# Decode steps that take keys and values together, and a fixed TensorE order beside the projections

## The chip, the cores and the metric

The kernel runs on one core of a Trainium2 chip. The metric is the time of one execution on the device in microseconds; the median of several executions counts, and less is better. TensorE (PE in the rows) multiplies matrices, its weight loads are listed apart as PEld; VectorE (DVE), ScalarE (ACT) and GpSimd (POOL) do the elementwise work; SyncE (SP) issues the DMAs, in order.

## The reference, cut to what matters

One layer of a streaming encoder, for 1024 prompt tokens and for a decode batch of 8 sequences with 16 new tokens each (128 rows that ride along as a ninth token tile). Group A has 8 heads of stick-breaking attention over the full past, group B 8 heads of softmax attention over the newest 512 past rows. The decode batch reads its past from caches in memory: 1024 rows of keys and as many of values for each sequence in group A, 512 in group B.

```python
q_a, k_a, v_a, q_b, k_b, v_b = split_heads(h, w_in)          # h = rmsnorm(x)
ka = jnp.concatenate([past_sb_k, k_a], axis=1)                # decode, group A
va = jnp.concatenate([past_sb_v, v_a], axis=1)
z = einsum('bqhd,bkhd->bhqk', q, k) * HEAD_DIM ** -0.5
log_keep = where(causal, log_sigmoid(-z), 0.0)
between = cumsum(log_keep, axis=3, reverse=True) - log_keep
w = where(causal, exp(log_sigmoid(z) + between), 0.0)
a = einsum('bhqk,bkhd->bqhd', w, v)
# group B: softmax(q k / 8 + relative bias) v; then per-head norms, the output
# projection, a SwiGLU feed-forward, a gated embedding and a final norm
```

## The kernel before

The kernel is one program whose stages are generators that call one another's steps. The projection `qkv` (L216) yields after each unit of 24 matmuls (8 blocks of the contraction by three products of high and low parts, `mm3`, L104). It goes through twelve column blocks of w_in: keys, queries and values of group A first, then keys, values and queries of group B. Its helper `others` (L244) handles keys and values: three token tiles of 24 matmuls each into one bank each of `ps["o"]`, a copy of each into `st`, and behind the third tile a tail: for keys six transposes (L260), the split into two parts and their writes; for values three casts and subtractions (`sv`, L264 to L268) and their writes; then the writes of the kernel's outputs. It yields after the first two tiles and after the tail.

`decode` (L314) is the other generator. Its setup loads the new queries, keys and values. Then it works through a list `seq` (L349 to L351) of pieces of 256 cached rows: key pieces and value pieces by turns, a batch's values following its keys by `nkc + VLAG` places (six in group A, three in group B). Group A has 32 key and 32 value pieces, group B 16 and 16. `fetch` loads a piece of 512 KB into one of seven buffers (six in group B), six (five) pieces ahead. `prepare` (L360) runs two pieces ahead: for keys eight transposes (L383) and two copies into `kT`, for values two transposes of the weights, three for a batch's first piece (`flip`, L389 to L394) and a copy into `wt`. `scores` (L397) multiplies four head pairs with 32 columns of queries each (L406) into one bank, `ps["s"]`; for the last piece of a batch in group A one matmul of 128 columns adds the causal mask (L409); two sigmoids on ScalarE read the bank. `weights` (L418) makes the scan and product on VectorE and the block `wn` of new weights on GpSimd. `outputs` (L440) multiplies two blocks of values (three for a batch's first piece) for four head pairs with 32 columns each (L449) into `acc`. Each fp32 matmul of 32 columns has two records in the trace, so a piece of keys shows 8 and a piece of values 16 or 24.

The order on each engine is set by a planner, which simulates the program and orders each engine's instructions ahead of time; on the chip every engine runs its own list in order. `tc.manual_schedule(engines=...)` makes the named engines keep the program's order instead. Before, decode's stages are all the planner's.

`advance(main, side, ratio, steps)` (L707) runs one step of `main` and then as many of `side` as the ratio makes due. The projection runs alone for 36 steps (L737). Group A's decode then runs beside 30 projection steps at 2.2 pieces per step (L747), and what is left of it runs out behind (L748). The stage's pools close, and prompt attention (`attention`, L492) starts beside the last 30 projection steps (L758). Group B's decode runs beside attention, and the embedding projection `embed` with it: `along` (L802) takes 0.55 embedding steps per decode piece, and attention takes 1.3 of both per step, for 40 steps (L816, L817).

Of the kernel before, what the change touches and what calls it, by code (L numbers as in the profile page):

```python
# [30 lines left out]
NEG = -1e30  # L31
LATE = 2
SKEW = 2
LAG, RAWS, PT = 5, 7, 2
VLAG, AHEAD = (2, 1), 2

# [2 lines left out]
def tile_hymba_step(  # L39
# [176 lines left out]
    def qkv(ch, hT, stg):  # L216
# [27 lines left out]
        def others(grp, w, c, wts, gs):  # L244

            wh, wl = wts
            for g in gs:
                st = stg.tile([P, 3, 256], F32, name="st", tag="st", bufs=2)
                for o in range(3):
                    ps_ = ps["o"].tile([P, 256], F32, name="ps", tag="O")  # L250
                    for k in range(KT):
                        mm3(ps_, *hT.tok(g * 3 + o, k), wh[:, k], wl[:, k], k == 0, k == KT - 1)
                    (V.tensor_copy if o % 2 else A.copy)(st[:, o], ps_)
                    if o < 2:
                        yield
                if w == 1:
                    for pr in range(2):
                        pt = ps["t"].tile([P, 384], F32, name="pt", tag="T")
# [21 lines left out]
                if g == 2:  # L280
# [1 line left out]
                        kv_sample[grp, w][0, :, :, c * 4 : c * 4 + 4, :].rearrange("b i h d -> (b i) (h d)"),  # L282
                        st[:, 2],
                    )
                yield

        loads = [(0, 1, 0), (0, 1, 1), (0, 0, 0), (0, 0, 1), (0, 2, 0), (0, 2, 1),
                 (1, 1, 0), (1, 1, 1), (1, 2, 0), (1, 2, 1), (1, 0, 0), (1, 0, 1)]
# [25 lines left out]
    def decode(grp, ch, dk):  # L314
# [79 lines left out]
            A.copy(wt, pt[:, : len(srcs) * P].rearrange("p (n m) -> p n m", m=P))  # L394
            return wt

        def scores(st, c, kT):  # L397
            last = c == nkc - 1
            nk = 272 if last else 256
            own = slice(c * 256, c * 256 + nk)  # L400
            q, w = st["q"], st["w"][:, own]
            sc = ps["s"].tile([P, 512], F32, name="sdec", tag="S")[:, :nk]

            masked = grp == 0 and last
            for pr in range(4):
                T.matmul(sc[pr * 32 : pr * 32 + 32], lhsT=q[:, pr], rhs=kT[:, pr, :nk], start=True, stop=not masked)  # L406
            if grp == 0:
                if masked:
                    T.matmul(sc[:, 256:], lhsT=identb, rhs=causalb, start=False, stop=True)  # L409
                A.activation(w, sc, AF.Sigmoid)  # L410
                A.activation(st["keep"][:, own], sc, AF.Sigmoid, scale=-1.0)
            else:
                mx = dk.tile([P, 1], F32, name="mx", tag="mx", bufs=4)
                V.tensor_tensor_reduce(w, sc, bias[:, own], 1.0,
                                       3e38 if st["mx"] is None else st["mx"], ALU.add, ALU.min, accum_out=mx)
                st["mx"] = mx
# [36 lines left out]
        def finish(st):  # L453
# [12 lines left out]
            V.tensor_scalar(ow, on, r[:, 0:1], None, op0=ALU.mult)  # L466
            nc.sync.dma_start(mixs[grp][b * 16 : b * 16 + 16, :].rearrange("i (h d) -> h i d", h=8), ow)

        ahead = ch.raws - 1
        for i in range(ahead):  # L470
            fetch(i)
        yield
        for i in range(AHEAD):
            prepare(i)
        for i, (kind, n, c) in enumerate(seq):
            if i + ahead < len(seq):
                fetch(i + ahead)
            if i + AHEAD < len(seq):
                prepare(i + AHEAD)
            x, wt = split.pop(i)  # L480
            if kind == "k":
                scores(batch[n], c, x)
                if c == nkc - 1:
                    weights(batch[n])
            else:
                outputs(batch[n], c, x, wt)
                if c == nkc - 1:
                    finish(batch[n])
            yield


# [252 lines left out]
    banks(dstack, "right", d=2, a=1)  # L744
    dp = pool(first, "dA", "left")
    dec = decode(0, Chunks(dp, "d", 1024, RAWS, 2), dp)
    advance(project, dec, 2.2, 30)  # L747
    for _ in dec:  # L748
        pass
    first.close()  # L750
    dstack.close()

# [49 lines left out]
    def along(a, b, ratio):  # L802

        due = 0.0
        for _ in a:
            yield
            due += ratio
            while due >= 1.0:
                due -= 1.0
                if next(b, "end") != "end":  # L810
                    yield
        yield from b

    next(dec)
    advance(att, dec, 0, 6)
    beside = along(dec, embed(), 0.55)  # L816
    advance(att, beside, 1.3, 40)  # L817
    for _ in beside:
        pass
    dstack.close()  # L820
# [655 lines left out]
```

## Time and profile before

| | us |
|---|---|
| median of three runs | 1763.65 (1763.17 to 1764.24) |
| the profiled execution | 1761.44 |
| its span, first to last instruction | 1759.7 |
| mean granted TensorE clock | 0.985 |
| TensorE busy | 1688.2 (96%) |
| VectorE busy | 1051.2 (60%) |
| GpSimd busy | 804.7 (46%) |
| ScalarE busy | 761.6 (43%) |

The profile is of one execution, with times in microseconds from its first instruction. Busy time counts an instruction from its start to its modelled end, so overlapping matmuls are seen best by their starts: the difference of two starts in the timeline is what an instruction costs TensorE. The timeline merges neighbours of one kind: "x8" are eight records. "128*32" says that the stationary operand has 128 rows and 32 columns. A bracket at a row's end is the idle time before it and what ended it. The granted clock is 1.00 for 2.4 GHz and 0.50 for 1.2 GHz, averaged over a stretch.

### The profile page before, as it was taken

To read this page: it belongs to the slowest core of one execution; us is meant where nothing else is said; L and a number is where in the kernel's file an instruction comes from. 1 tells how busy PE (TensorE), PEld (TensorE's weight loads), DVE (VectorE), ACT (ScalarE), POOL (GpSimd) and SP (SyncE) were. 2 spreads that over 40 slices of the span, in tenths; PEclk is the share of its full clock that TensorE was granted. 3 is DMA by queue.
4 is the path that set the end of the run, shared out by engine and by line. 5 is a ranking of instruction groups with operands and counts; after the bars stand their busy time and mean duration, and the time that the engine had idled before them with its cause. 6 is when DMAs were issued, how large, how long until landed. Compare 5 with 4: busy or idle time off the path is not lost.

```text
span 1759.7 us, 29028 instructions
## 1 busy us (share of the span) xinstructions
PE 1688.2 (96%) x11048; PEld 1469.3 (84%) x11048; DVE 1051.2 (60%) x1638; ACT 761.6 (43%) x1646; POOL 804.7 (46%) x635
## 2 busy tenths in 40 slices
PE   7999999999996899899989999999999999999998
PEld 7998888889995687787868888888888788887998
DVE  5212444257778566653686666666666598878635
ACT  5213434367766567743553333333233333333532
POOL 3214321277559322312345555555555465558354
PEclk9999999999998899999999999999999999999999
DMA  6756887656468696855422222222222684411123
GB/s 210 252 187 201 292 270 267 187 159 171 137 173 232 199 264 196 222 169 187 163 83 90 93 93 93 93 93 92 95 93 93 235 327 138 138 51 60 48 80 138
DMA packets 183467, 279.93 MB, mean 159 GB/s; under 512 B 15264, under 2 KB 115232, under 8 KB 181920
## 3 DMA queue, kind: packets, MB, share of 16 engines
q1 hardware_dynamic: 183328, 278.07, 49.4%
q8 instruction: 88, 1.44, 0.3%
q14 instruction: 51, 0.42, 0.1%
HBM read 198.47 MB, written 79.56 MB: 158 GB/s over the span
## 4 chain that ended last, share of the span: by engine, by line
PE 86%; DMA 4%; DVE 4%; POOL 3%; ACT 2%; issue 1%; SPq 0%; POOLq 0%; ACTq 0%; DVEq 0%
PE ps L998 19%; PE ps L105 9%; PE ps L106 9%; PE ps L107 8%; PE pt L1249 6%; PE ps L1249 4%; PE pt L998 3%; PE pt L584 3%; PE pt L383 2%; PE acc L449 2%; PE po L608 2%; PE po L607 2%; PE S L551 2%; PE sdec L406 1%; DMA v<-sv 1%
## 5 line engine op out<-in xcount | busy, mean ns | idle before, releaser
L110 POOL TENSOR_TENSOR wlo<-wraw,whi 128x512 fp32r<-128x512 f32 (+1 forms) x128 | 232.7, 1846 | 233.1 <-ACT whi L149 228.8
L105 PE MATMUL ps<-whi,hTh 128*128 128x256 f32 x576 | 168.9, 293 | 1.0 <-ACT sq L222 0.6
L106 PE MATMUL ps<-wlo,hTh 128*128 128x256 f32 x576 | 165.9, 288 | 1.0 <-POOL wlo L110 1.0
L107 PE MATMUL ps<-whi,hTl 128*128 128x256 f32 x576 | 166.6, 289 | 0.0
L149 ACT CAST whi<-wraw 128x512 fp32r<-128x512 f32 (+1 forms) x132 | 90.4, 749 | 98.0 <-PE ps L998 65.7
L565 DVE TENSOR_TENSOR_SCAN keep<-keep,zero 128x128 f32<-128x128 f32 (+4 forms) x64 | 100.9, 1585 | 38.5 <-ACT keep L557 37.8
L566 POOL TENSOR_TENSOR w<-w,keep 128x127 f32<-128x127 f32 (+4 forms) x64 | 89.2, 1405 | 66.4 <-DVE keep L565 57.9
L105 PEld LDWEIGHTS ps<-whi,hTh 128*128 128x128 f32 x576 | 110.9, 193 | 7.2 <-issue 5.0
L110 DVE TENSOR_TENSOR wtl<-pt,wth 128x512 fp32r<-128x512 f32 (+1 forms) x192 | 94.7, 514 | 32.0 <-ACT wth L588 31.1
L106 PEld LDWEIGHTS ps<-wlo,hTh 128*128 128x128 f32 x576 | 110.9, 192 | 3.2 <-issue 1.8
L107 PEld LDWEIGHTS ps<-whi,hTl 128*128 128x128 f32 x576 | 111.0, 193 | 0.3 <-issue 0.2
L584 PE MATMUL pt<-ident,w 128*128 128x128 f32 x528 | 92.0, 286 | 17.2 <-POOL w L566 13.5
L588 ACT CAST wth<-pt 128x512 fp32r<-128x512 f32 (+1 forms) x192 | 84.4, 464 | 37.8 <-PE pt L584 37.4
L584 PEld LDWEIGHTS pt<-ident,w 128*128 128x128 f32 x528 | 64.4, 146 | 27.1 <-POOL w L566 14.3
L105 PE MATMUL ps<-whi,hVh 128*128 128x256 f32 x288 | 81.8, 284 | 0.5 <-ACT hVh L1396 0.5
L106 PE MATMUL ps<-wlo,hVh 128*128 128x256 f32 x288 | 81.7, 284 | 0.0
L607 PE MATMUL po<-wth,vk 128*128 128x256 f32 (+1 forms) x304 | 80.7, 294 | 1.0 <-DVE wtl L110 1.0
L107 PE MATMUL ps<-whi,hVl 128*128 128x256 f32 x288 | 81.5, 284 | 0.0
L551 PE MATMUL S<-qk 128*128 128x384 f32 (+2 forms) x192 | 73.5, 385 | 4.7 <-DVE mxp L560 1.7
L608 PE MATMUL po<-wtl,vk 128*128 128x256 f32 (+1 forms) x304 | 77.0, 294 | 0.0
L384 DVE COPY kT<-pt 128x512 f32<-128x512 f32 x48 | 32.9, 688 | 65.9 <-PE pt L383 59.7
L110 POOL TENSOR_TENSOR actl<-actr,acth 128x1024 fp32r<-128x1024 f32 (+1 forms) x22 | 56.5, 2571 | 33.9 <-DMA sr<-acts 18.2
(351 smaller groups left out, 5402.6 us busy)
## 6 DMA issues: line engine op xcount, KB each, us to landing
draw<-in_cache_sb_k SPq DMA_DIRECT2D x32, 512.0 KB
draw<-in_cache_sb_v SPq DMA_DIRECT2D x32, 512.0 KB
act<-sg SPq DMA_DIRECT2D x11, 1152.0 KB
actr<-act SPq DMA_DIRECT2D x22, 576.0 KB
wraw<-in_w_in SPq DMA_DIRECT2D x12, 1024.0 KB
wraw<-in_w_gate SPq DMA_DIRECT2D x11, 1024.0 KB
wraw<-in_w_up SPq DMA_DIRECT2D x11, 1024.0 KB
v<-sv SPq DMA_DIRECT2D x36, 256.0 KB
```

The source lines that it names most:

```text
L105: T.matmul(out, lhsT=ah, rhs=bh, start=start, stop=False)
L106: T.matmul(out, lhsT=ah, rhs=bl, start=False, stop=False)
L107: T.matmul(out, lhsT=al, rhs=bh, start=False, stop=stop)
L110: eng.tensor_tensor(out, a, hi.bitcast(F32), op=ALU.subtract)
L149: A.copy(h[:, o], v[:, o])
L551: T.matmul(sc, lhsT=hd["qq"][:, qs], rhs=hd["kkh"][:, kc], start=True, stop=False)
L565: V.tensor_tensor_scan(rev, rev, zero[:, 0:1].to_broadcast([P, n]), 1.0, op0=ALU.mult, op1=ALU.add)
L584: T.transpose(pt[:, (c - c0) * P : (c - c0 + 1) * P], w[:, c * P : (c + 1) * P], ident)
L607: T.matmul(dst, lhsT=vs, rhs=wth[:, kb - base, c0:c1], start=(i == 0), stop=False)
L608: T.matmul(dst, lhsT=vs, rhs=wtl[:, kb - base, c0:c1], start=False, stop=(i == nkb - 1))
L998: T.matmul(out, lhsT=a[x][:, k], rhs=b[y][:, k], start=(not more and k == 0 and n == 0), stop=(k == 3 and n == 2), skip_group_check=more)
L1249: T.matmul(out, lhsT=a[i][:, x, m * P : (m + 1) * P], rhs=b[j][:, x], start=(not more and x == 0 and n == 0), stop=(x == 1 and n == 2), sk ...
```

## The change

Decode goes by steps instead of pieces: one place of the list, with a key piece, a value piece or both. In a step come the fetches, the preparations of the next step's pieces, scores and outputs, and then what follows a batch's last piece (`weights`, `finish`). The mask is added by four matmuls of 32 columns each. `others` yields behind each tile, the third one ahead of its tail. TensorE keeps the program's order in group A's decode stage. The ratios go from 2.2 to 1.2 (group A), from 0.55 to 1.0 and from 1.3 to 1.0 (group B).

```diff
+R2 = 1.2
...
                     (V.tensor_copy if o % 2 else A.copy)(st[:, o], ps_)
-                    if o < 2:
-                        yield
+                    yield
                 if w == 1:
...
-                yield
 
         loads = [(0, 1, 0), (0, 1, 1), (0, 0, 0), (0, 0, 1), (0, 2, 0), (0, 2, 1),
...
-        def scores(st, c, kT):
+        def scores(st, c, kT, _):
...
                 if masked:
-                    T.matmul(sc[:, 256:], lhsT=identb, rhs=causalb, start=False, stop=True)
+                    for pr in range(4):
+                        o = slice(pr * 32, pr * 32 + 32)
+                        T.matmul(sc[o, 256:], lhsT=identb[:, o], rhs=causalb, start=False, stop=True)
...
+        steps, at = [], 0
+        for pieces in zip_longest(ks, vs):
+            n = sum(x is not None for x in pieces)
+            steps.append(range(at, at + n))
+            at += n
         ahead = ch.raws - 1
         for i in range(ahead):
             fetch(i)
         yield
-        for i in range(AHEAD):
+        for i in steps[0]:
             prepare(i)
-        for i, (kind, n, c) in enumerate(seq):
-            if i + ahead < len(seq):
-                fetch(i + ahead)
-            if i + AHEAD < len(seq):
-                prepare(i + AHEAD)
-            x, wt = split.pop(i)
-            if kind == "k":
-                scores(batch[n], c, x)
+        for j, step in enumerate(steps):
+            for i in step:
+                if i + ahead < len(seq):
+                    fetch(i + ahead)
+            for i in steps[j + 1] if j + 1 < len(steps) else ():
+                prepare(i)
+            for i in step:
+                kind, n, c = seq[i]
+                (scores if kind == "k" else outputs)(batch[n], c, *split.pop(i))
+            for i in step:
+                kind, n, c = seq[i]
                 if c == nkc - 1:
-                    weights(batch[n])
-            else:
-                outputs(batch[n], c, x, wt)
-                if c == nkc - 1:
-                    finish(batch[n])
+                    (weights if kind == "k" else finish)(batch[n])
             yield
...
-    advance(project, dec, 2.2, 30)
-    for _ in dec:
-        pass
+    with tc.manual_schedule(engines={mybir.EngineType.PE}):
+        advance(project, dec, R2, 30)
+        for _ in dec:
+            pass
...
-    beside = along(dec, embed(), 0.55)
-    advance(att, beside, 1.3, 40)
+    beside = along(dec, embed(), 1.0)
+    advance(att, beside, 1.0, 40)
```

## Rows read from the trace of the kernel before

**Rows 1.** The page: busy time of each engine, and the chain that ended last, by engine.
```profile
PE 1688.2 (96%) x11048; PEld 1469.3 (84%) x11048; DVE 1051.2 (60%) x1638; ACT 761.6 (43%) x1646; POOL 804.7 (46%) x635
...
PE 86%; DMA 4%; DVE 4%; POOL 3%; ACT 2%; issue 1%; SPq 0%; POOLq 0%; ACTq 0%; DVEq 0%
```

**Rows 2.** Busy time by stretch: the stretch, its length, then each engine's busy time and instructions, the granted clock, the share of the DMA engines and GB/s. The first is group A's decode beside the projections, the last is group B's decode beside attention.
```profile
150.00:345.00 195.00, 192.13 (x2060) 163.59 (x2058) 70.85 (x101) 80.10 (x207) 54.57 (x72) 1.00 0.76 248
345.00:400.00 55.00, 51.15 (x380) 47.32 (x381) 32.92 (x38) 33.84 (x86) 35.27 (x27) 0.94 0.56 163
...
500.00:600.00 100.00, 78.93 (x566) 68.16 (x565) 68.04 (x106) 60.23 (x144) 61.00 (x54) 0.88 0.69 195
...
565.00:712.00 147.00, 136.84 (x1198) 108.89 (x1198) 92.90 (x292) 93.45 (x247) 42.55 (x69) 0.97 0.75 218
```

**Rows 3.** TensorE's timeline in group A's decode: the last projection matmuls before a stretch of scores, then a key piece and a value piece with their transposes, then the projection again; and two neighbouring groups of single transposes. Columns: start, length, engine, line, operation, out<-in, form, count.
```profile
154.57 0.28 PE L107 MATMUL ps<-whi,hTl 128*128 128x256 f32 x1
154.78 0.64 PE L406 MATMUL sdec<-kT,qbd 128*32 128x256 f32 x8
...
205.97 0.64 PE L406 MATMUL sdec<-kT,qbd 128*32 128x256 f32 x8
206.54 0.44 PE L392 MATMUL pt<-ident,wdec 128*128 128x128 f32 x2
206.91 0.64 PE L449 MATMUL acc<-draw,wt 128*32 128x128 f32 x16
207.49 0.39 PE L105 MATMUL ps<-whi,hTh 128*128 128x256 f32 x1
207.71 0.28 PE L106 MATMUL ps<-wlo,hTh 128*128 128x256 f32 x1
207.83 0.28 PE L107 MATMUL ps<-whi,hTl 128*128 128x256 f32 x1
...
212.09 0.27 PE L392 MATMUL pt<-ident,wn 128*128 128x128 f32 x1
212.20 0.38 PE L392 MATMUL pt<-ident,wdec 128*128 128x128 f32 x2
```

**Rows 4.** The same timeline where a value piece and a key piece follow each other with nothing between.
```profile
235.13 0.64 PE L449 MATMUL acc<-draw,wt 128*32 128x128 f32 x16
235.59 0.61 PE L406 MATMUL sdec<-kT,qbd 128*32 128x256 f32 x8
236.13 0.44 PE L392 MATMUL pt<-ident,wdec 128*128 128x128 f32 x2
```

**Rows 5.** The same timeline: two value pieces in one stretch, and the last stretch of group A's decode. From the one at 154.78 (rows 3) to this last one there are 60 stretches of 128*32 rows with 128*128 rows between them.
```profile
313.76 1.08 PE L449 MATMUL acc<-draw,wt 128*32 128x128 f32 x32
314.78 0.39 PE L105 MATMUL ps<-whi,hTh 128*128 128x256 f32 x1
...
323.85 1.08 PE L449 MATMUL acc<-draw,wt 128*32 128x128 f32 x32
```

**Rows 6.** The same timeline: a batch's last key piece with its mask.
```profile
219.77 0.67 PE L406 MATMUL sdec<-kT,qbd 128*32 128x272 f32 x8
220.37 0.18 PE L409 MATMUL sdec<-causalb,identb 128*128 128x16 bf16 x1
220.41 0.36 PE L105 MATMUL ps<-whi,hTh 128*128 128x256 f32 x1
```

**Rows 7.** TensorE's timeline in group B's decode: the first stretch, value pieces cut by attention's matmuls, and the last stretch. From the first to the last there are 42 stretches.
```profile
567.96 0.64 PE L406 MATMUL sdec<-kT,qbd 128*32 128x256 f32 x8
...
641.70 0.63 PE L449 MATMUL acc<-draw,wt 128*32 128x128 f32 x12
...
642.63 0.41 PE L449 MATMUL acc<-draw,wt 128*32 128x128 f32 x2
642.97 0.66 PE L584 MATMUL pt<-ident,w 128*128 128x128 f32 x4
...
709.44 0.42 PE L449 MATMUL acc<-draw,wt 128*32 128x128 f32 x6
```

**Rows 8.** Who waited for whom: total, times and longest in us. TensorE from 150 to 345, ScalarE from 140 to 345, TensorE from 345 to 400.
```profile
PE sdec L406 <- ACT keep L411: 1.5, 1, 1.5
...
ACT sv L267 <- DMA v<-sv: 13.4, 7, 4.6
...
PE pt L584 <- POOL w L566: 3.2, 1, 3.2
```

**Rows 9.** Timelines of TensorE, VectorE, GpSimd and ScalarE: a batch's masked scores, then its scan and its block of new weights; and the copy of a projection tile.
```profile
201.07 0.18 PE L409 MATMUL sdec<-causalb,identb 128*128 128x16 bf16 x1
...
202.01 2.33 DVE L424 TENSOR_TENSOR_SCAN keep<-keep,zero 128x1040 f32<-128x1040 f32 x1 [0.74 <-ACT keep L411]
...
205.77 0.20 POOL L437 COPY wn<-wdec 128x16 f32<-128x16 f32 x1 [3.77 <-DVE wdec L425]
...
205.21 0.37 ACT L253 COPY st<-ps 128x256 f32<-128x256 f32 x1 [2.96 <-PE ps L107]
```

**Rows 10.** Busy time by stretch of 20 us (columns as in rows 2): the one with the most DMA in group A's decode, and one at the start of attention.
```profile
200.00:220.00 20.00, 20.00 (x227) 16.00 (x229) 7.76 (x12) 9.79 (x25) 4.58 (x10) 1.00 0.92 312
...
360.00:380.00 20.00, 16.47 (x107) 14.89 (x106) 10.89 (x10) 12.24 (x31) 19.01 (x11) 0.83 0.44 139
```

**Rows 11.** Timelines of TensorE and SP from the end of group A's decode to attention's first matmul.
```profile
324.86 0.44 PE L260 MATMUL pt<-ident,st 128*128 128x128 f32 x2
325.05 0.36 PE L105 MATMUL ps<-whi,hTh 128*128 128x256 f32 x1
...
333.21 0.52 SPq L508 DMA_DIRECT2D qk<-qT0h  x1
...
342.83 0.47 PE L551 MATMUL S<-qk 128*128 128x128 f32 x2 [1.11 <-DMA qk<-kT0h]
```

## The prediction

> **What bounds the kernel now.** I read the page's busy table and chain first: TensorE is busy 96% of the span and carries 86% of the chain that ended last [rows 1]. Next the table by stretch: from 150 to 345 us, where group A's decode runs beside the projections, TensorE is busy 192.1 of 195 us at full clock; in group B's decode it is busy 136.8 of 147 [rows 2]. So an edit counts by TensorE time saved, if nothing new makes TensorE wait. Then TensorE's timeline shows what one decode step costs [rows 3]. Decode's matmuls write 32 partitions at a time (128*32 in the rows), everything else is 128*128, and going from one form to the other costs time that the rows show plainly.
>
> **The price of a stretch of 32-column matmuls.** A projection matmul starts every 0.12 us (207.71 to 207.83). After a stretch the first one takes 0.22 (207.49 to 207.71): 0.10 to leave. Before a stretch, the last one takes 0.21 (154.57 to 154.78): 0.09 to enter. Two transposes between two stretches take 0.37 (206.54 to 206.91), against 0.22 for two at 0.11 each (212.09 to 212.20 shows one): 0.15 for leaving and entering together. The stretch has a fixed part as well: eight score matmuls alone take 0.57 (205.97 to 206.54) and sixteen output matmuls alone 0.58, but both back to back take 1.00 (235.13 to 236.13), not 1.15 [rows 3, 4]. So each stretch that is joined to another saves 0.15 and one leaving and entering: 0.30 where transposes stood between, 0.34 where projection matmuls did. I take 0.32.
>
> **Group A.** By the program, before has 64 pieces (32 of keys, 32 of values). The timeline from the first to the last shows them in 60 stretches [rows 5]. In the change, 32 key pieces and 32 value pieces with six steps of lag make 38 steps, 26 of them with both. The order on TensorE is now the program's: next step's transposes first, then scores, then outputs, so 38 steps are 38 stretches, and 37 as nothing stands between the last two. 23 fewer at 0.32: **-7.4 us**.
>
> The mask: eight times, one 128*128 matmul of 16 columns (0.04 from 220.37 to 220.41, the leaving is paid behind it anyway) becomes four of 128*32 [rows 6]. A 32-column matmul of 16 columns is not in the trace. Nearest rows: sixteen more output matmuls in one stretch cost 1.02 - 0.58 = 0.44, 0.027 each [rows 3, 5], so four cost 0.11, and 8 x (0.11 - 0.04) = **+0.6**. Ends: -0.3 if they cost nothing; +2.4 if each four cost 0.34, as a stretch of two output matmuls by itself does (642.63 to 642.97) [rows 7]. I take +0.6, since they stand inside a stretch. The rows say 0.027 us for one more tile in a stretch. The Trainium skill's page "TensorE: Matmul & The Clock Gate", section "Measured speedup vs the span model", gives about 4 ns for a further tile of a packed group; by that the masks would cost some 0.1 us in all and not 0.9, an estimate from that page, and the sum would be 0.8 us lower. The measured row decides here.
>
> The fixed order: nothing else may fill when TensorE's next instruction waits. What is late next? (a) Scores need kT, copied one step earlier, and the one score bank, freed by two sigmoids; today one such wait of 1.5 us is left in the whole stage [rows 8]. (b) The first output step of a batch needs scan, product and wn: 202.01 to 205.97, 4.9 us after the masked scores end at 201.1 [rows 9]. The change leaves the rest of a step, at least one projection step (24 x 0.12 = 2.9 us) and another decode step (ten transposes at 0.11, 1.0 and 0.2 for entering and leaving: 2.3) before the flip that reads it: some 5.7 us, enough but barely when two decode steps follow each other. (c) Outputs now precede the scan's emission, which costs that chain 0.5 us of its room. (d) ScalarE waits 13.4 us in seven pieces for the DMA that frees a v tile, the longest 4.6 [rows 8]; behind such a wait stand the copies of kT and wt and the sigmoids, and TensorE waits for those. A decode step and a projection step (5 us) cover the single wait; without that cover it is TensorE's. Bounds 0 and 13.4; I take **+1.5**, the wait that the stage shows today, since the planned order is already close to the program's there [rows 3, 4].
>
> The moved yield: the third block's transposes (L260), its split and its DMAs on SP now come behind a decode step instead of in front of it. On TensorE this gives the copy of the third PSUM block (0.4 us) [rows 9] 2.3 us of cover that the fixed order would otherwise have lacked; on SP the cache fetches of that step go ahead of the block's writes. Who waits: v's sample rows for new_v, first needed by the first output step, six steps later. Zero, and at most the 1.5 above if the cover goes.
>
> Ratio 2.2 to 1.2: 30 projection steps take 35 advances, setup and 34 steps; four value-only steps follow alone at about 0.95 us each (0.37 + 0.58). It is TensorE work that before did between projections, so it costs nothing by itself. DMA demand rises with the shorter stage: its share is 0.76 over the stage and 0.92 in the worst 20 us [rows 2, 10], and 195 us less 5 raises it by 3%. Zero, above 1.0 in the worst slice only.
>
> **Group B.** 19 steps stand for 32 pieces, and the trace shows 42 stretches: the planner cuts output groups into twos and sixes with attention matmuls between [rows 7]. There TensorE's order stays the planner's. Kept whole: 23 fewer, -7.4. All cut again: 0. I take eleven fewer, about half: the pieces fall from 32 to 19, but the attention work that cuts them is still there, and for 10 us of this stretch TensorE idles anyway [rows 2]. 11 x 0.32 = **-3.5**. The ratios 0.55/1.3 to 1.0/1.0: 38 decode and embedding steps over 40 attention steps instead of 51 single ones; the same keys and values per attention step, zero.
>
> **The stage changes.** Between 345 and 400 TensorE idles 3.9 us and from 500 to 600 21 us with the clock at 0.88 [rows 2]: waits for POOL and DMA that a new plan will shuffle. After group A's last output (324.86) attention's first loads are issued at 333.21 behind the write of the last decode result, and its first matmul starts at 342.83; six projection steps fill TensorE till then [rows 11]. They are still there after the change. Zero, bounds -4 and +4 (about the 3.9 of the first).
>
> **Sum.** -7.4 + 0.6 + 1.5 - 3.5 = -8.8 us. The profiled execution takes 1761.44 (span 1759.7 and 1.7 around it): 1752.6. The median of the runs lies 2.2 higher, so 1763.65 - 8.8 = **1754.9**, with its own range 1750 to 1760.
>
> **Rivals.** *Fixed order turns ScalarE's waits into TensorE's* (slower). Place: projection steps 37 to 48, whose v blocks make ScalarE wait for DMA. All 13.4 us arrive and TensorE falls to the lower clock level: in 360 to 380 us a wait of 3.2 us for POOL goes with a granted clock of 0.83, 6.8 us at 1.2 instead of 2.4 GHz, 3.4 us lost [rows 8, 10]. -7.4 + 0.6 + 13.4 + 3.4 - 3.5 = +6.5: 1770. It decides against the change once more than 10.3 us of waits come through. For: order can't adapt, one score bank. Against: the order of before is nearly the same and waits 1.5 us. The Trainium skill's page "TensorE: Matmul & The Clock Gate", section "HAM oscillation — how this bites in real kernels", says the same of a TensorE that idles between bursts; the slice with 0.83 agrees. Chance 0.14.
>
> *The gain of A is given back at the stage change* (no change). The four value-only steps push decode's end behind the last projection step; if the plan doesn't hoist projection steps over attention's loads, up to 18 us (324.86 to 342.83) lie open, of which some 5 would eat A's net 5.3; with B at 0 to -3.5 the time is 1760 to 1764, 1762 in the middle. It would be the same if the change didn't do what it says, that is, if transposes came to lie between scores and outputs again; in A the fixed order speaks against that, in B nothing does. Chance 0.18.
>
> *B joins fully and waits shrink*: -7.4 + 0.6 - 7.4, less 1.5 us of waits that go: -15.7, 1748. For: steps emit scores and outputs together. Against: the cuts in [rows 7]. Chance 0.14. The forecast keeps 0.54.
>
> **Chances.** A measurement can tell about 0.2%, 3.5 us. Faster by more: forecast and full join, 0.68; within: 0.18; slower: 0.14. The range leaves out half of the slower case and the far end of the full join: 1746 to 1767.
>
> **What would show it.** In the profile after: 37 stretches in group A's decode, each with sdec directly followed by acc in about 1.0 us (1.2 with nv); four small masks inside; TensorE busy all through; the stage (first sdec to attention's first S) about 5 us shorter. In B, fewer acc groups of two and six. Wrong if TensorE shows new waits for ACT or DVE in A, if sdec and acc back to back still take 1.15, or if what A gains is lost between 340 and 600.

## The result, and the profile after

| | before | after |
|---|---|---|
| median, us | 1763.41 (1762.86 to 1764.24, 4 runs) | 1752.72 (1748.87 to 1754.20, 4 runs) |
| ratio, with 95% interval | | 0.9936 (0.9918 to 0.9953) |
| profiled execution; its span | 1761.44; 1759.7 | 1754.20; 1752.4 |
| mean granted TensorE clock | 0.985 | 0.984 |

The change is faster by 10.7 us; the forecast was 8.8. The profiled execution of after is the slowest of its four, and that of before lies below its four, so their spans differ by less, 7.3. The page of after, busy time by engine and the chain that ended last, by engine [rows 1]:

```profile
PE 1678.7 (96%) x11072; PEld 1470.8 (84%) x11072; DVE 1048.3 (60%) x1638; ACT 764.0 (44%) x1646; POOL 806.1 (46%) x635
...
PE 84%; DMA 5%; DVE 4%; ACT 2%; POOL 2%; issue 1%; SPq 1%; POOLq 0%; DVEq 0%; ACTq 0%
```

TensorE is busy 9.5 us less, with 24 more records (8 masks of four instead of one). It has more instructions and needs less time, which is what the price of a stretch says.

TensorE's timeline of after: a whole step, a masked step, and the last stretch of group A's decode [rows 3, 5, 6]:

```profile
215.17 1.03 PE L382 MATMUL pt<-ident,draw 128*128 128x128 f32 x8
216.04 0.27 PE L391 MATMUL pt<-ident,wn 128*128 128x128 f32 x1
216.15 0.38 PE L391 MATMUL pt<-ident,wdec 128*128 128x128 f32 x2
216.46 0.64 PE L405 MATMUL sdec<-kT,qbd 128*32 128x256 f32 x8
216.92 0.62 PE L450 MATMUL acc<-draw,wt 128*32 128x128 f32 x16
217.47 0.38 PE L106 MATMUL ps<-whi,hTh 128*128 128x256 f32 x1
...
305.39 0.67 PE L405 MATMUL sdec<-kT,qbd 128*32 128x272 f32 x8
305.87 0.19 PE L410 MATMUL sdec<-causalb,identb 128*32 128x16 bf16 x4
305.90 0.62 PE L450 MATMUL acc<-draw,wt 128*32 128x128 f32 x16
306.45 0.39 PE L106 MATMUL ps<-whi,hTh 128*128 128x256 f32 x1
...
322.73 1.08 PE L450 MATMUL acc<-draw,wt 128*32 128x128 f32 x32
```

Scores and outputs lie together: from 216.46 to 217.47 it is 1.01 us, as the prediction read it from the rare neighbours in before (1.00). From the first stretch at 156.40 to the last at 322.73 there are 37, the number forecast. The masked step costs 1.06, four masks included: they take 0.03 us, from 305.87 to 305.90.

Where the 7.3 us between the two spans arise, by the same events in each trace:

| | before | after | difference so far |
|---|---|---|---|
| attention's first matmul | 342.83 | 334.68 | -8.2 |
| group B's first scores | 567.96 | 558.12 | -9.8 |
| group B's last output matmul starts | 709.6 | 697.8 | -11.8 |
| end of the span | 1759.7 | 1752.4 | -7.3 |

So 8.2 us come in group A's stage, 1.7 from there to group B's decode, 2.0 in its stage, and 4.5 are given back later, in this execution. Two more profiles of the changed kernel, below, keep the first part (334.90, 335.42) and give back 1.2 and 4.2.

Who waited for whom: TensorE, and then ScalarE, in group A's stage of after (total, times, longest) [rows 8]:

```profile
PE pt L382 <- ACT kT L383: 0.7, 2, 0.5
PE pt L382 <- DVE kT L383: 0.6, 1, 0.6
PE pt L382 <- DVE sq L111: 0.3, 1, 0.3
...
ACT sv L267 <- DMA v<-sv: 6.9, 4, 2.3
```

TensorE's three waits make 1.6 us. ScalarE still waits for the DMA that frees v, 6.9 instead of 13.4 us, and nothing of it reaches TensorE: the last of these waits ends at 151.41, ahead of the first copy into kT at 154.63.

Busy time by stretch of after, columns as in [rows 2]: group A's stage, the start of attention, and group B's stage:

```profile
150.00:345.00 195.00, 193.06 (x2150) 171.80 (x2148) 73.24 (x110) 84.69 (x214) 50.90 (x70) 1.00 0.81 258
345.00:400.00 55.00, 51.88 (x402) 48.49 (x402) 37.14 (x43) 39.45 (x102) 43.77 (x32) 0.97 0.63 185
555.00:699.00 144.00, 133.05 (x1174) 108.61 (x1174) 91.77 (x284) 91.48 (x242) 37.89 (x66) 0.94 0.76 219
```

In group A's stage TensorE idles 1.9 of 195 us, as the waits say. At the start of attention the granted clock is 0.97 instead of 0.94; in group B's stage it is lower than before, 0.94 for 0.97. What is given back lies partly at the far end. The same view of a stretch of 70 us that begins 160 us ahead of the end, in before, in after, and in another execution of the changed kernel (after_again):

```profile
1600.00:1670.00 70.00, 67.84 (x425) 60.85 (x424) 50.29 (x73) 29.74 (x61) 38.54 (x32) 1.00 0.12 36
```

```profile
1592.00:1662.00 70.00, 67.82 (x415) 60.69 (x413) 49.62 (x72) 29.22 (x59) 37.36 (x32) 0.98 0.10 32
```

```profile
1586.00:1656.00 70.00, 67.84 (x422) 60.64 (x420) 51.01 (x73) 29.81 (x60) 38.94 (x33) 1.00 0.11 32
```

The granted clock is 1.00, 0.98 and 1.00. 0.02 of 70 us is 1.4 us of the 3.3 by which after's rest is longer than after_again's.

### The profile page after: what moved, and what is told of

Same layout as the page of the kernel before. It is cut to its first block, busy times and chain, and to the rows that moved or that the text cites. A ratio compares the mean times of both kernels' runs of the same rounds, so it can differ in the third digit from the quotient of the medians.

```text
span 1752.4 us, 29092 instructions
## 1 busy us (share of the span) xinstructions
PE 1678.7 (96%) x11072; PEld 1470.8 (84%) x11072; DVE 1048.3 (60%) x1638; ACT 764.0 (44%) x1646; POOL 806.1 (46%) x635
## 3 DMA queue, kind: packets, MB, share of 16 engines
q8 instruction: 88, 1.44, 0.3%
## 4 chain that ended last, share of the span: by engine, by line
PE 84%; DMA 5%; DVE 4%; ACT 2%; POOL 2%; issue 1%; SPq 1%; POOLq 0%; DVEq 0%; ACTq 0%
PE ps L1005 19%; PE ps L106 9%; PE ps L107 9%; PE ps L108 9%; PE pt L1256 6%; PE ps L1256 5%; PE pt L1005 3%; PE pt L590 3%; PE pt L382 2%; PE po L614 2%; PE S L557 2%; PE po L613 2%; PE acc L450 1%; PE sdec L405 1%; PE S L558 1%
## 5 line engine op out<-in xcount | busy, mean ns | idle before, releaser
L111 DVE TENSOR_TENSOR wtl<-pt,wth 128x512 fp32r<-128x512 f32 (+1 forms) x192 | 94.0, 513 | 24.2 <-ACT wth L594 23.5
L383 DVE COPY kT<-pt 128x512 f32<-128x512 f32 x48 | 33.0, 688 | 57.0 <-PE pt L382 46.5
```

The source lines that it names most:

```text
L111: eng.tensor_tensor(out, a, hi.bitcast(F32), op=ALU.subtract)
```

## The experiments

The theory from the prediction: the time comes from 32-column matmuls that lie together, about 0.32 us for each stretch saved, and TensorE's fixed order matters only as it keeps them together. The rivals: the fixed order or the later yield brings the time by itself; group B brings it; or what A gains is lost at the stage change. The runs came in three groups of four, each beside runs of before on the same chip: 1763.78 us (17 runs) for after_again, flip_between, planner_a and fixed_only, 1762.72 (17) for a_only, old_yield, wide_mask and fixed_b, 1764.30 (11) for the others. Each time is a median with its range and count. "Stretches" counts those of 128*32 rows in the profiled execution, in group A / group B (before: 60 / 42). "First S" is attention's first matmul there (before: 342.83; after: 334.68).

| run | us | ratio to before (95%) | stretches | first S |
|---|---|---|---|---|
| after_again | 1751.42 (1748.20 to 1751.88, 5) | 0.9929 (0.9916 to 0.9941) | 37 / 33 | 334.90 |
| after_third | 1751.47 (1749.70 to 1756.82, 6) | 0.9930 (0.9913 to 0.9947) | 37 / 33 | 335.42 |
| flip_between | 1761.14 (1759.08 to 1764.11, 11) | 0.9985 (0.9977 to 0.9994) | 63 / 33 | 343.78 |
| planner_a | 1751.12 (1748.92 to 1753.09, 5) | 0.9930 (0.9916 to 0.9944) | 49 / 33 | 337.31 |
| fixed_only | 1771.72 (1767.49 to 1774.75, 6) | 1.0044 (1.0029 to 1.0059) | 63 / 42 | 355.67 |
| pairs_only | 1755.82 (1754.43 to 1757.74, 6) | 0.9950 (0.9935 to 0.9965) | 67 / 33 | 346.02 |
| a_only | 1756.07 (1751.96 to 1757.28, 5) | 0.9953 (0.9940 to 0.9965) | 37 / 41 | 336.58 |
| old_yield | 1755.85 (1753.33 to 1762.13, 5) | 0.9951 (0.9938 to 0.9963) | 37 / 33 | 348.48 |
| wide_mask | 1749.67 (1748.07 to 1751.02, 4) | 0.9922 (0.9909 to 0.9935) | 44 / 33 | 336.31 |
| wide_mask_again | 1752.80 (1751.37 to 1756.87, 6) | 0.9936 (0.9920 to 0.9952) | 44 / 33 | 337.37 |
| fixed_b | 1766.73 (1757.88 to 1772.06, 12) | 1.0018 (1.0003 to 1.0032) | 37 / 19 | 335.33 |
| double_a | 1774.98 (1769.09 to 1778.18, 6) | 1.0054 (1.0034 to 1.0074) | 20 / 33 | 352.44 |

### The changed kernel again (after_again, after_third)

No edit. These stand beside the others of their group.

> The changed kernel once more, as the measure for the others on the same chip. Both theories: 1752.7 us, between 1748.9 and 1754.2 as its runs showed, 10.7 below before.

> The changed kernel, as the measure for this call: 1752, between 1748 and 1755.

The medians are 12.4 and 12.8 us below before. In group A they repeat within 0.8 us (first S at 334.68, 334.90, 335.42); behind group B's decode (whose last matmul starts at 697.8, 695.1, 696.1) the three spans still differ, 1752.4, 1746.4 and 1750.3. The part from there to the end takes 1054.6, 1051.3 and 1054.2 us, and 1050.1 in before. It is not the change's own: fixed_only, whose decode goes by pieces like before's, takes 1054.3 there, and flip_between and planner_a 1051.8 and 1051.4. In all fourteen profiles the clock of the stretch shown above is 1.00 in the four where this part is shortest (before, after_again, planner_a, flip_between; 1050.1 to 1051.8) and 0.98 in the other ten (1051.8 to 1055.2). So differences of some 5 us between single profiled executions mean nothing unless one stage shows them.

### Same steps, transposes between scores and outputs (flip_between)

```diff
-            for i in steps[j + 1] if j + 1 < len(steps) else ():
+            todo = list(steps[j + 1]) if j + 1 < len(steps) else []
+            for i in [i for i in todo if grp or seq[i][0] == "k"]:
                 prepare(i)
-            for i in step:
+                todo.remove(i)
+            for x, i in enumerate(step):
+                if todo and (x or len(step) == 1):
+                    prepare(todo.pop())
...
+            for i in todo:
+                prepare(i)
```

> The changed kernel with one move: in group A's steps with both pieces the next value piece's transposes stand between scores and outputs. Same instructions, same fixed order otherwise, 63 stretches of 32-column matmuls instead of 37. Joined stretches pay: 26 x 0.30 = 7.8 us slower than the changed kernel, 1760.5, attention's first matmul 7 to 8 us later (342). The fixed order pays by itself, or the stage changes were merely shuffled well: no difference of more than 2 us from the changed kernel, 1753.

Group A keeps its steps, fixed order, ratio and yield; only the two or three transposes of the weights move from ahead of the scores to behind them. TensorE's timeline of flip_between:

```profile
218.42 0.64 PE L405 MATMUL sdec<-kT,qbd 128*32 128x256 f32 x8
218.99 0.33 PE L391 MATMUL pt<-ident,wn 128*128 128x128 f32 x1
219.15 0.38 PE L391 MATMUL pt<-ident,wdec 128*128 128x128 f32 x2
219.46 0.64 PE L450 MATMUL acc<-draw,wt 128*32 128x128 f32 x16
220.04 0.39 PE L106 MATMUL ps<-whi,hTh 128*128 128x256 f32 x1
```

The same work lies in two stretches: 0.57 and 0.58 us instead of 1.01 together, and the first transpose behind scores takes 0.16 (218.99 to 219.15) instead of 0.11. There are 26 stretches more, and attention starts 8.9 us later than in after_again: 0.34 each. TensorE waits 2.7 us in this stage instead of 1.6; without these 1.1 it is 0.30 each, the figure of the expectation. The median, 1761.14, is the expected time within a microsecond; it is 9.7 us above after_again's, where 7.8 were expected. The run also says what the rest of the change is worth in group A: with 63 stretches first S is at 343.78; before has 60 and 342.83, three more stretches at 0.32 are 1.0, and the waits are alike (2.7, and 2.6 in before [rows 8, 11]). Fixed order, ratio and yield together come to nothing there.

### The planner's order in group A's stage (planner_a)

```diff
-    with tc.manual_schedule(engines={mybir.EngineType.PE}):
-        advance(project, dec, R2, 30)
-        for _ in dec:
-            pass
+    advance(project, dec, R2, 30)
+    for _ in dec:
+        pass
```

> The changed kernel without the fixed order in group A's decode stage. Joined stretches pay: the planner finds scores and outputs of a step ready together and keeps most of them together, since before it made only 60 stretches of 64 pieces; 38 to 44 stretches, 0 to 2 us slower than the changed kernel, 1752.7 to 1755. The fixed order pays by itself: most of the gain of group A is lost, 1759 to 1761, with waits of TensorE in the stage.

As fast as the changed kernel. TensorE's timeline of planner_a, one step that the planner cuts and one that it leaves whole:

```profile
250.75 0.64 PE L405 MATMUL sdec<-kT,qbd 128*32 128x256 f32 x8
251.32 0.66 PE L382 MATMUL pt<-ident,draw 128*128 128x128 f32 x4
251.90 0.64 PE L450 MATMUL acc<-draw,wt 128*32 128x128 f32 x16
...
257.14 0.64 PE L405 MATMUL sdec<-kT,qbd 128*32 128x256 f32 x8
257.60 0.62 PE L450 MATMUL acc<-draw,wt 128*32 128x128 f32 x16
```

The number of stretches was missed: 49, where 38 to 44 were expected. In the stage this shows, as first S comes 2.4 us later than in after_again: twelve stretches more at 0.32 are 3.8, and the 1.6 us of waits under the fixed order are gone, since TensorE is busy for 195.0 of 195 us here; that makes 2.2. In the median (1751.12 against 1751.42) it does not, and the ranges overlap. So the fixed order is not needed for the result; at most it is worth a couple of microseconds in its own stage.

### The fixed order alone (fixed_only)

The kernel before, with one edit:

```diff
-    advance(project, dec, 2.2, 30)
-    for _ in dec:
-        pass
+    with tc.manual_schedule(engines={mybir.EngineType.PE}):
+        advance(project, dec, 2.2, 30)
+        for _ in dec:
+            pass
```

> The kernel before, with TensorE's order fixed in group A's decode stage and nothing else. Joined stretches pay: 60 stretches become 63 or 64, 3 x 0.3 = 1 us, and the tail of a key block, no longer behind a decode step, makes TensorE wait for a copy (0.4 us and the signals, six times in keys): 1764 to 1768, not faster than before. The fixed order pays by itself: 1755 to 1758.

Slower by 7.9 us, and by more than expected. TensorE's waits in group A's stage of fixed_only:

```profile
PE pt L383 <- ACT kT L384: 3.8, 1, 3.8
PE pt L383 <- DVE sq L110: 2.2, 2, 1.4
PE pt L392 <- POOL wn L437: 1.5, 2, 0.8
PE pt L260 <- ACT st L253: 1.2, 5, 0.2
```

The longest, 3.8 us up to 156.81, is what the prediction's slower rival described. ScalarE's timeline shows its copy into kT right behind casts that waited for the DMA that frees v (3.58 us, and 1.44 once more):

```profile
152.50 0.41 ACT L267 CAST sv<-st 128x256 fp32r<-128x256 f32 x1 [3.58 <-DMA v<-sv]
155.87 0.40 ACT L267 CAST sv<-st 128x256 fp32r<-128x256 f32 x1 [1.44 <-DMA v<-sv]
156.18 0.58 ACT L384 COPY kT<-pt 128x512 f32<-128x512 f32 x1
```

A low clock went with it, as the rival had it: from 140 to 165 us the granted clock is 0.86, where before has 1.00; 0.14 of 25 us is 3.5 us, some of it while TensorE waited. The other waits are shorter: the program's order leaves too little between a copy or a block of new weights and TensorE's use of it. With the changed kernel's steps and its yield the same fixed order waits 1.6. First S is 12.8 us later than before; three more stretches make 1.0 of it, the waits 7.1 (8.7, and 1.0 of attention's first matmul for its load, less the 1.5 and 1.1 that before has there [rows 8, 11]) and the clock up to 3.5. Some 1 to 2 us stay unassigned.

### Only the steps (pairs_only)

Of the whole change only the steps and the ratios stay: the planner's order, the yield behind the tail and the wide mask of before.

```diff
-    with tc.manual_schedule(engines={mybir.EngineType.PE}):
-        advance(project, dec, R2, 30)
...
+    advance(project, dec, R2, 30)
...
+                    if o < 2:
+                        yield
...
+                yield
...
-                    for pr in range(4):
-                        o = slice(pr * 32, pr * 32 + 32)
-                        T.matmul(sc[o, 256:], lhsT=identb[:, o], rhs=causalb, start=False, stop=True)
+                    T.matmul(sc[:, 256:], lhsT=identb, rhs=causalb, start=False, stop=True)
```

> The change without the fixed order, without the moved yield and with the wide mask: the steps and the ratios alone, all orders the planner's. Joined stretches carry the change: 1752 to 1755, at least three quarters of the gain. The moved yield is needed even under the planner: 1756 or more.

The median is at the edge between the two expectations, and the trace decides. In group A the planner has 67 stretches, more than before, and first S is at 346.02, 3.2 us later than before: nothing is gained there. TensorE has no waits in the stage; seven more stretches (2.2) and eight more projection matmuls ahead of first S (1.0), less the 2.6 us of waits of before, explain 0.6 of the 3.2. TensorE's timeline of pairs_only shows how outputs are cut:

```profile
235.02 0.62 PE L450 MATMUL acc<-draw,wt 128*32 128x128 f32 x10
235.57 0.66 PE L384 MATMUL pt<-ident,draw 128*128 128x128 f32 x4
236.16 0.41 PE L450 MATMUL acc<-draw,wt 128*32 128x128 f32 x2
```

The last two output matmuls cost 0.34 (236.16 to the next row of transposes at 236.50), where two inside a stretch cost 0.05. What pairs_only gains comes from group B and the stage change, where its 33 stretches are those of the changed kernel; from first scores to last outputs group B takes 132.9 us, before 141.6. That steps are emitted together is not enough in group A: something must keep them whole. Between planner_a's 49 and these 67 lie two edits, the yield and the mask, and which of them keeps the planner's steps whole was not separated.

### Group A alone (a_only)

Group B goes by pieces again, with the old loop and the old ratios.

```diff
+        if grp:
+            for i in range(AHEAD):
+                prepare(i)
+            for i, (kind, n, c) in enumerate(seq):
+                if i + ahead < len(seq):
+                    fetch(i + ahead)
...
+                yield
+            return
...
-    beside = along(dec, embed(), 1.0)
-    advance(att, beside, 1.0, 40)
+    beside = along(dec, embed(), 0.55)
+    advance(att, beside, 1.3, 40)
```

> The changed kernel with group B's decode as before: pieces by turns, ratios 0.55 and 1.3. Joined stretches pay in both groups: group B goes from 33 stretches back to about 42, 9 x 0.32 = 2.9 us slower than the changed kernel, 1755 to 1756. Only group A's part counts, since TensorE idles in group B's stretch anyway: no difference, 1752.7.

Faster than before by 6.7 us, with group B's 41 stretches. Group B's stage takes 143.6 us here and 141.6 in before; with the steps it takes 139.7, 136.3 and 136.9 in the three profiles of the changed kernel. So the steps in B, with their ratios, are worth about 4 us or more of the stage in these profiles. Not all of it is the price of stretches: TensorE idles 13.0 us of the stage in a_only, and 8.9, 9.4 and 11.1 in the three. And one stage alone is not sharp: with the same steps and 33 stretches it takes 132.9 in pairs_only. The two halves don't add up exactly: group A with B undone 6.7, pairs without A's gain 8.5, both 12.8 beside it.

### The yield behind the tail again (old_yield)

```diff
-                    yield
+                    if o < 2:
+                        yield
...
+                yield
```

> The changed kernel with the projection's tail ahead of the decode step again, as before. If the moved yield only lends cover: on TensorE six key tails wait for the third tile's copy, 0.4 us and the signals, some 0.6 each, 3 to 4 us slower than the changed kernel, 1756. If the yield is of no account: no difference, 1752.7.

A ratio of 0.9951, where the changed kernel has 0.9929 and 0.9930: 4 us less is gained (6.9 us below its own before in the medians, where those are 12.4 and 12.8, so 4 to 6). The profiled execution was the slowest of five. TensorE's waits in group A's stage of old_yield:

```profile
PE pt L384 <- DVE sq L111: 5.6, 5, 2.2
PE pt L261 <- ACT st L254: 1.2, 5, 0.2
```

Under the fixed order the key block's tail runs ahead of the decode step: its transposes (L261) wait for the copy of the third tile, and the decode transposes behind them wait for VectorE to read the PSUM bank that the tail's transposes filled. With the later yield a decode step stands ahead of the tail and a projection step behind it. So it is a cover, as the prediction had it, and it is worth 4 to 6 us, not the 1.5 given as its most. In the profiled execution first S is 13.6 us later than in after_again. The waits (these and three of 2.0 together, 8.8) less the 1.6 of after explain 7.2 of it. Twenty more projection matmuls stand ahead of first S, 2.4 at 0.12. From 260 to 280 us the granted clock is 0.91, 1.8 us. The last 2.2 stay open.

### One wide mask (wide_mask, wide_mask_again)

```diff
-                    for pr in range(4):
-                        o = slice(pr * 32, pr * 32 + 32)
-                        T.matmul(sc[o, 256:], lhsT=identb[:, o], rhs=causalb, start=False, stop=True)
+                    T.matmul(sc[:, 256:], lhsT=identb, rhs=causalb, start=False, stop=True)
```

> The changed kernel with the mask as one matmul of 128 columns again. Joined stretches pay: seven steps with both pieces are cut in two and the eighth leaves 32 columns twice, 7 x (0.15 + 0.09 + 0.10) less the 8 x 0.06 of the narrow masks: 2 us slower than the changed kernel, 1754.7. Rival, that a change of number format or of tile inside a stretch costs as much as leaving it: no difference, 1752.7.

> The changed kernel with the wide mask, repeated beside the changed kernel. Its stage in group A ended 1.4 us later, with 44 stretches instead of 37, and yet the whole was 1 to 2 us shorter. If that 1.4 us is lost in the end as well: 1 to 2 us slower than the changed kernel. If the start of attention hides it: equal within 1.5 us. If the wide mask is truly better further on: faster by 1 us or more again.

The time does not tell the two masks apart: 1749.67 in one group, 1752.80 beside after_third's 1751.47 in the other. The trace does. Seven of the eight masks stand between scores and outputs (the first batch's has no outputs yet), and the wide one cuts the stretch: 44 instead of 37. TensorE's timeline of wide_mask, the step shown above in after:

```profile
306.63 0.67 PE L405 MATMUL sdec<-kT,qbd 128*32 128x272 f32 x8
307.23 0.18 PE L408 MATMUL sdec<-causalb,identb 128*128 128x16 bf16 x1
307.35 0.65 PE L448 MATMUL acc<-draw,wt 128*32 128x128 f32 x16
307.92 0.39 PE L106 MATMUL ps<-whi,hTh 128*128 128x256 f32 x1
```

It takes 1.29 us instead of 1.06, and seven times 0.23 are 1.6; first S comes 1.4 to 2.0 us later (336.31 and 337.37 against 334.90 and 335.42). By attention's 65th score matmul this is gone (406.65 against 406.71 in after_again, 407.68 against 406.96 in after_third, where 0.7 is left). Busy time by stretch, the start of attention, in after_again and under it in wide_mask:

```profile
345.00:420.00 75.00, 71.35 (x547) 67.03 (x548) 52.34 (x60) 54.67 (x137) 55.77 (x39) 0.98 0.59 173
```

```profile
345.00:420.00 75.00, 71.42 (x559) 66.80 (x558) 52.98 (x63) 54.49 (x137) 56.82 (x40) 1.00 0.62 176
```

The granted clock is 1.00 with the wide mask, in both of its profiles, and 0.98 in all three of the changed kernel. 0.02 of 75 us is 1.5 us, the size of what is lost before. The wide mask pays 1.6 us at its place, and in these two profiles most or all of it comes back where attention starts. It is not the start's time alone: a_only and planner_a, with first S at 336.58 and 337.31, have 0.98 as well. Nor is it the mask alone: pairs_only has the wide mask and 0.98, before has it and 0.95, fixed_only has it and 1.00. Why the clock holds in some of them was not tried.

### Fixed order in group B too (fixed_b)

```diff
-    advance(att, beside, 1.0, 40)
-    for _ in beside:
-        pass
+    with tc.manual_schedule(engines={mybir.EngineType.PE}):
+        advance(att, beside, 1.0, 40)
+        for _ in beside:
+            pass
```

> The changed kernel with TensorE's order fixed in group B's decode stage as well. Joined stretches pay there too: 33 stretches become 19, 14 x 0.32 = 4.5 us faster, 1748. Rival, that the planner's freedom is worth more beside attention, whose matmuls wait for VectorE, ScalarE and GpSimd (23 us of waits between 500 and 715): new waits of more than 5 us, 1755 to 1775.

Nineteen stretches, as few as there are steps, and the whole gain is gone (1.0018): 15 us above the changed kernel for 14 stretches fewer. TensorE's waits in group B's stage of fixed_b, above 2 us:

```profile
PE pj L106 <- DVE mx L415: 7.1, 2, 3.6
PE S L557 <- DVE mxp L566: 6.7, 2, 5.8
PE sdec L405 <- DVE kT L383: 3.3, 1, 3.3
PE S L557 <- ACT pjo L799: 2.9, 8, 0.7
```

The stage takes 149.8 us, 10 to 14 more than with the planner's order; TensorE idles 18.0 us of it instead of 8.9 to 11.1, and the granted clock is 0.92 instead of 0.94 to 0.98. The rival of this run was right: in the program's order TensorE waits for VectorE and ScalarE, in decode (L383, L415), attention (L566) and the embedding (L799), and the cuts that the planner makes are cheaper than these waits.

### Two steps in one stretch (double_a)

Group A's steps are taken in pairs: two key pieces, then two value pieces, with a lag of eight pieces, four buffers for keys and four for values, a second score bank, and in its place one bank less for the transposes of the weights.

```diff
-R2 = 1.2
+R2 = 0.7
...
-VLAG, AHEAD = (2, 1), 2
+VLAG, AHEAD = (4, 1), 2
...
+            for j, p in enumerate(pairs):
+                if j + 1 < len(pairs):
+                    early(pairs[j + 1])
+                for x in "kv":
+                    for i in p:
+                        kind, n, c = seq[i]
+                        if kind == x:
+                            (scores if kind == "k" else outputs)(batch[n], c, *split[i])
```

> The changed kernel with two steps of group A's decode taken together: two score banks and one bank for the turned weights, four buffers each for keys and values, values eight places behind their keys instead of six, ratio 0.7. Joined stretches pay at any size: 20 stretches instead of 37, 17 x 0.32 = 5.4 us faster than the changed kernel, 1746, first attention matmul at about 330. Rival, that bigger lumps of transposes wait for the copies of their banks and for the sigmoids: no faster, 1752 or more, with new waits of TensorE in the stage.

Twenty stretches, 17 fewer than the change, and 23.5 us slower than after_third. TensorE's waits of double_a in group A's stage, and its busy time there:

```profile
PE pt L387 <- ACT kT L388: 5.6, 7, 2.7
PE pt L396 <- ACT wt L398: 4.5, 5, 1.5
PE pt L396 <- DMA vraw<-in_cache_sb_v: 2.9, 2, 2.5
...
PE pt L387 <- DVE kT L388: 1.6, 2, 1.2
```

```profile
150.00:345.00 195.00, 178.69 (x2027) 158.03 (x2026) 66.77 (x103) 79.83 (x204) 43.63 (x67) 1.00 0.72 238
```

TensorE idles 16.3 of 195 us, after 1.9. Some twenty transposes in a row outrun the copies behind them, and those of the weights (L396) have one bank where they had two. The decode also starts 9 us late (first scores at 166.0, in after_again at 156.6): its longest wait, 2.7 us for a copy into kT, again has ScalarE waiting 2.25 us for the DMA that frees v just before that copy. The loads come in pairs of another order as well. The 14.4 us of added idle time are not all of the 17.0 by which first S is later than in after_third, the less so as 17 stretches fewer should have saved 5.4. The run shows that longer stretches cost more than they save in this form, not that they must.

## Why the prediction was right

**The price of a stretch** held: 0.32 was taken, and flip_between measures 0.30 to 0.34 for 26 of them, without and with the waits that came with them. **The count in group A** was exact, 37. This term, -7.4, is the core of the result: flip_between, which keeps all else of the change, loses it, and planner_a shows that the fixed order isn't needed for it. pairs_only shows that the steps under the planner are not enough without the yield and the narrow masks; which of the two it takes is open.

**The mask** was costed at +0.6, and that was the wrong row. The prediction took 0.027 us for a narrow matmul from output matmuls of 128 columns; the masks have 16, and four of them take 0.03 together, 0.008 each. That is 8 x (0.03 - 0.04), nothing. The Trainium skill's page "TensorE: Matmul & The Clock Gate", section "Measured speedup vs the span model", with its 4 ns for each further tile, was nearer for these short ones (8 ns measured); for the output matmuls the trace stays at 27. What the sum did not say is that the wide mask would have cut seven stretches: the narrow ones spare 1.6 us in the stage, of which the end shows none.

**The fixed order's stalls** were forecast at +1.5, and TensorE waits 1.6 in the stage. But the sum kept the waits of before and added these; the 1.5 for `keep` and the 1.1 for attention's first load [rows 8, 11] are gone in after. That is most of why group A's stage gained 8.2 where -7.4 + 0.6 + 1.5 = -5.3 was forecast: -7.4 for the stretches, +1.6 for the new waits and -2.6 for the old make -8.4, and the three profiles give 8.2, 7.9 and 7.4. Waits under a fixed order are real: fixed_only has 8.7 us of them, old_yield 8.8, fixed_b more; the rival's own chain, from the DMA that frees v over ScalarE to TensorE and its clock, shows in fixed_only and, at full clock, in double_a. In the changed kernel ScalarE's last such wait lies ahead of the first copy into kT. That longer steps avoid waits is not shown, as old_yield has them; what avoids most of them is **the moved yield**, which was forecast at zero with a bound of 1.5 if its cover goes; old_yield puts it at 4 to 6 us. That bound was too small, though the term itself (zero, while the cover stands) was right.

**Group B** was forecast at 31 stretches by an even split between all joined and none; 33 are there. Nine at 0.32 are 2.9; its stage got shorter by 2.0, 5.3 and 4.8 us in the three profiles. Its waits and its clock moved as well (from first scores to last outputs 0.96 in before, 0.94, 0.98 and 0.98 in the three), so the size is right and its parts are not separated. The rival of a full join needed an order that the planner doesn't give, and fixed_b shows what that order costs.

**The stage change** was put at zero within 4 and gave 1.3 to 1.7: from attention's first matmul to group B's first scores it is 225.1 us before and 223.4 to 223.9 after. The low clock at attention's start is shorter (0.97 for 0.94 from 345 to 400 us). **The ratio** cost nothing, as forecast: first S in flip_between stands where the stretches alone put it.

**What was not forecast** is the far end: behind group B's decode, whose code did not change, 1.2 to 4.5 us are given back in the profiles. The clock of one stretch there goes with it, and it does so in kernels with and without the change, so it may be the executions that differ; before was profiled once, and this stays open. That the total came out near is thus in part luck: group A gained 2 to 3 us more than its terms said, and the far end, which had no term, gave back 1.2 to 4.5. No version ran that beats the changed kernel by more than the runs differ; planner_a and the wide mask equal it.

## What to carry to other kernels

Count how often TensorE changes between narrow and full-width matmuls, read the price of one change from the starts in the timeline, and put narrow pieces side by side wherever they belong to the same step: here some 0.3 us each, with more instructions and less time. Fix an engine's order by hand only where each instruction's input is ready well before its turn: the same fixed order was harmless with the later yield, 4 to 6 us dearer without it, cost 8 us over single pieces, and 15 in group B beside attention. When a saving at one place does not reach the end, look at the granted clock behind it before looking for a lost wait.

## What the hardware showed that was not expected

- A further 128*32 record inside a stretch cost about 0.008 us with 16 columns in bf16 (four in 0.03) and 0.027 with 128 in fp32 (sixteen in 0.44); whether columns or format make the difference was not separated.
- Two output matmuls by themselves between transposes cost 0.34 us, six times as much as two in a stretch (0.054).
- In two stretches the granted clock took few values: at attention's start, from 345 to 420 us, it was 0.95 in before, 1.00 in fixed_only and in both profiles of the changed kernel with the wide mask, and 0.98 in the other ten; over the 70 us that begin 160 us ahead of the end it was 1.00 in four profiles and 0.98 in ten, with no edit near it.
